# A ten-stage kernel on one core: half splits taken from GpSimd, the convolution's tables in their own tile, the last expert rows in two tiles

## The chip, the cores and the metric

The kernel runs on one core of one Trainium2 chip. Its engines are TensorE (PE in the profile; PEld is its weight load), VectorE (DVE), ScalarE (ACT), GpSimd (POOL) and SyncE (SP), which issues most of the transfers. The metric is the time on the device in microseconds, the median of several runs. Before the change it is 1920.85 us, the median of 1922.42, 1920.85 and 1916.68.

## The reference

One batch of 256 tokens with 1024 features goes through two blocks of two layers each. Everything is float32.

```python
def first_block(x, ...):
    for layer in range(2):
        mix = conv_mixers(x, ...) if layer % 2 == 0 else stick_breaking_attention(x, ...)
        x = layer_norm(DEEPNORM_ALPHA * x + mix, ...)
        ffn = hierarchical_moe(x, ...)   # 32 experts of hidden width 512, 2 of them for each token
        x = layer_norm(DEEPNORM_ALPHA * x + ffn, ...)
    return x

def conv_mixers(x, w_in, conv_a, conv_b_w, conv_b_bias, norm_b_g, norm_b_b, w_out):
    a_b, a_c, a_v, b_val, b_gate = jnp.split(x @ w_in, ...)
    y_a = a_b * causal_depthwise_conv(a_c * a_v, conv_a)              # width 3
    g = b_val * jax.nn.sigmoid(b_gate)
    g = causal_depthwise_conv(g, conv_b_w) + conv_b_bias              # width 31
    y_b = jax.nn.silu(layer_norm(g, norm_b_g, norm_b_b))
    return jnp.concatenate([y_a, y_b], axis=-1) @ w_out
```

The second block does for each of its two layers, with an RMS norm ahead of each part: an attention mixer (layer 0 two kinds of heads, block attention and dilated windows; layer 1 a mixer, NSA, with compressed, selected and windowed keys and values, weighted by gates), a SwiGLU layer of width 2816, and a gated embedding (PLE): `x + sigmoid(norm(x) @ w_gate) * (p @ w_proj)`.

## The kernel before

There are ten stages, one after the other: 0 the convolution mixer, 1 experts, 2 stick-breaking attention, 3 experts, 4 the first attention mixer of the second block, 5 SwiGLU, 6 embedding gate, 7 NSA mixer, 8 SwiGLU, 9 embedding gate and output. By the trace they begin at about 0, 119, 590, 709, 1182, 1297, 1493, 1525, 1697 and 1889 us.

**Weights and halves.** Weights come as items of 1 MB by SyncE's queue (`pump`, L202), each into the next free one of a few rotating buffers. A matmul in float32 is done in three passes (`mm3`, L397 to L399) of operands that were split into a high and a low part, and so each dense item is split before use, half by half. ScalarE copies the high part of a half (`wh`, L237) and `split_to` has the low one (`wl`) subtracted at L248, on GpSimd if the flag `on_pool[0]` is set and else on VectorE:

```python
            eng = G if on_pool[0] else V
            eng.tensor_tensor(out=lv, in0=src, in1=hv.bitcast(F32), op=OP.subtract)
```

**What sets the order.** Each unit of work on one half ends with `tick()`. It first runs whatever was put off to this tick with `later(n, f)`, n ticks after it was put off, and then splits ahead, up to three halves beyond the one in use:

```python
        while due and due[0][0] <= now[0]:
            heapq.heappop(due)[2]()
        split_to(limit(here[0] + 3))
```

Each engine runs its instructions in the order in which this program writes them. Four high and four low tiles rotate.

**Stage 0** (`conv_mix`). One tile `scr` of 128x2048 holds the rows of the convolutions' tables (`fvr`, 37 rows), the rows of all norms' vectors (`vr`, 14 rows) and, later, `yb` and `sq`. SyncE's queue loads them between weight items. TensorE transposes the tables at L601 (`vecs`) and the norms' vectors at L331 (`vectors`); x is transposed at L522.

**Experts** (stages 1 and 3). Each expert's hidden part goes through `ps<-w,xg` (L919) and its output (L941) is written to 32 rows of a tile `y4` that four experts share (`down`, L950 on VectorE and L952 on ScalarE). A last set of matmuls combines the rows of all experts per token (`combine`), and `Rows` normalises: `take` (L495) gathers statistics, `begin` (L499, L458) ends them, `shift` (L504) makes minus mean times rstd, and `end` writes x (L512, L514). At the end of stage 3 `lows` has the first split halves of stage 4 subtracted on GpSimd, and `Norm.put_all` writes `x` in feature order with its high and low parts (L1325, L1246 and L1248, L1251).

**Stage 2** (`stick_mix`) builds a mask from a tile `neg`, which shares its buffer with the tile `kt` of the cumulative masks (L1113).

**Embedding gates** (stages 6 and 9, `ple`). Eight units of one half each: 24 matmuls, then `gate` (L1644 on VectorE, a sigmoid on ScalarE) and, for the unit before, `finish` (L1649, L1650), after every second one the high and low part of x for the next stage (L1251). `on_pool` is set for every second unit.

**NSA mixer** (stage 7). After units for gates, queries and values come two turns of a loop over the head groups g = 2 and 3, with a unit for the group's queries (`q_unit`), steps of the attention of the earlier groups (`step`), and the scale of the queries (`qs`: `hsq`, L1381 to L1385). `on_pool` is set from this loop on until late in the output projection (`feat_out`).

Of the kernel before, what the change touches and what calls it, by code (L numbers as in the profile page):

```python
# [70 lines left out]
def tile_kernel(ctx: ExitStack, tc: tile.TileContext, A, out, first=0, last=9):  # L71
# [197 lines left out]
    due, now = [], [0, 0]  # L269

# [10 lines left out]
    def tick():  # L281
        now[0] += 1
        while due and due[0][0] <= now[0]:
            heapq.heappop(due)[2]()
        split_to(limit(here[0] + 3))
# [193 lines left out]
    class Rows:  # L479
# [17 lines left out]
        def begin(self):  # L497
            self.mv = sm.tile([128, 2], F32, name="lnmv")
            V.bn_aggr(self.mv, self.st)  # L499
            self.r = rstd(self.mv[:, 1:2], LN_EPS, 1.0, "ln")  # L500

        def shift(self):
            self.nb = sm.tile([128, 1], F32, name="lnnb")
            V.scalar_tensor_tensor(self.nb, self.mv[:, 0:1], -1.0, self.r, op0=OP.mult, op1=OP.mult)  # L504
# [50 lines left out]
    def conv_mix():  # L555


        with tc.tile_pool(name="cm", bufs=1, reuse_waits="tile") as cp:
            wd = [c_tile(F32).rearrange("p (n f) -> p n f", f=32) for _ in range(2)]
            xh, xl = take_c(2)  # L560
            scr = cp.tile([128, 2048], F32, name="scr")
            fvr, vr = scr[0:37, 0:512], scr[0:14, 1024:2048]
            yb = scr[:, 1024:2048].rearrange("p (b t) -> p b t", b=4)
            sq = scr[:, 0:1024].rearrange("p (b t) -> p b t", b=4)
            pump(2)
            Q.dma_start(fvr[0:3, :], A["even_conv_a"][0])
            Q.dma_start(fvr[3:34, :], A["even_conv_b_w"][0])
            Q.dma_start(fvr[34:35, :], A["even_conv_b_bias"])
            Q.dma_start(fvr[35:36, :], A["even_norm_b_g"])
            Q.dma_start(fvr[36:37, :], A["even_norm_b_b"])  # L570
            pump(1)
            vectors = vector_loads(vr)
            prep = router_loads(0)
            pump()
            vec = cp.tile([128, 4, 37], F32, name="vec")
# [5 lines left out]
            gs = cp.tile([128, 2, 4, 28 + SEQ], F32, name="gs")  # L581
# [8 lines left out]
            for c in range(2):  # L590
                for kq in range(2):
                    v = turned(c, kq)
                    s = (slice(None), slice(4 * kq, 4 * kq + 4), slice(c * 128, (c + 1) * 128))
                    S.activation(xh[s], v, AF.Copy)
                    V.tensor_tensor(out=xl[s], in0=v, in1=xh[s].bitcast(F32), op=OP.subtract)
                split_to(c + 1)

# [22 lines left out]
            def shifted():  # L620

                for b in range(2):
                    ps = [bank()[:, 0:28 + SEQ] for _ in range(4)]
                    for s in range(4):
                        for c in range(4):
                            f = slice(32 * c, 32 * c + 32)
                            T.matmul(ps[c][32 * s:32 * s + 32], ident[f, f], gp[f, b, s:s + 28 + SEQ], start=True,
                                     stop=True)
                    for c in range(4):
                        if c % 2:  # L630
                            S.activation(gs[:, b, c, :], ps[c], AF.Copy)
                        else:
                            V.tensor_copy(gs[:, b, c, :], ps[c])

            def conv(i):
                ps = bank()
                for b in range(2):
                    for q in range(8):
                        for c in range(4):
                            T.matmul(ps[32 * c:32 * c + 32, b * SEQ:(b + 1) * SEQ], wd[i][:, (b * 4 + c) * 8 + q, :],  # L640
                                     gs[:, b, c, 4 * q:4 * q + SEQ], start=q == 0, stop=q == 7)
                for b in range(2):
                    S.activation(yb[:, 2 * i + b, :], ps[:, b * SEQ:(b + 1) * SEQ], AF.Identity,
                                 bias=vec[:, 2 * i + b, 34:35])
            later(2, vecs)
            later(3, tap_rows)
            later(3, vectors)
# [18 lines left out]
            kept = {}  # L666

            def b_sum():
                m = bank()
                for b in range(4):  # L670
# [5 lines left out]
            def b_stats():  # L676
                p2 = bank()
# [178 lines left out]
    def moe(layer):  # L856
        stage = 2 * layer + 1
        with tc.tile_pool(name="wd", bufs=ND, reuse_waits="tile") as wd, \
# [74 lines left out]
            def down(e):  # L933
# [11 lines left out]
                if ee == 0:  # L945
                    y4s[q] = hl.tile([128, D], F32, name="y4", tag="l")
                for c in range(4):
                    o, v = y4s[q][32 * ee:32 * ee + 32, c * 256:(c + 1) * 256], pd[32 * c:32 * c + 32, 0:256]
                    if e == NE - 1 and c % 2:
# [4 lines left out]
            def combine(q, cs=(0, 1)):  # L954
                for c in cs:
                    for n in range(2):
                        T.matmul(acc[2 * c + n], dwt[:, q % 2, c * 128:(c + 1) * 128],
                                 y4s[q][:, n * 512:(n + 1) * 512], start=q == 0, stop=q == 7)
# [117 lines left out]
            r[0].begin()  # L1076
# [4 lines left out]
            r[1].begin()  # L1081
            r[1].shift()
            r[1].end(dst[1], 1)
            def lows():
                on_pool[0] = True
                split_to(ahead)
# [11 lines left out]
    def stick_mix():  # L1098
        with tc.tile_pool(name="st", bufs=1, reuse_waits="tile") as cp, \
# [4 lines left out]
            neg = cw.tile([128, 128], F32, name="neg", tag="kt", bufs=1)  # L1104
# [128 lines left out]
    class Norm:  # L1233
# [20 lines left out]
        def put_all(self):  # L1254

            for k in (0, 2, 1, 3, 4, 6, 5, 7):
                self.high(k, k % 4 > 1)
            for k in range(8):
# [375 lines left out]
    def ple(cp, cw, pl, cur, nxt):  # L1634
# [18 lines left out]
        for k in range(8):  # L1653
# [7 lines left out]
            on_pool[0] = k % 2 == 1  # L1661
            tick()
        on_pool[0] = False
# [3 lines left out]
    def nsa_mix(bp, sl, cur, nxt):  # L1667
        with tc.tile_pool(name="ns", bufs=1, reuse_waits="tile") as cp, \
# [242 lines left out]
            on_pool[0] = True  # L1911
            for g in (2, 3):
                qs, turn_q = q_unit(g)
# [5 lines left out]
                turn_q()  # L1919
                if g == 2:  # L1920
                    later(1, step)
            step()
            step()
            nx = nxt()
# [134 lines left out]
```

## Time and profile before

| | |
|---|---|
| median of three runs | 1920.85 us |
| the profiled execution's own time | 1922.68 us |
| its span | 1921.0 us |
| mean granted TensorE clock | 0.903 |
| TensorE busy | 1631.7 us, 85% |
| VectorE busy | 740.4 us, 39% |
| ScalarE busy | 677.2 us, 35% |
| GpSimd busy | 122.1 us, 6% |
| moved by DMA | 559 MB, 291 GB/s |

The profile is of one execution. A row of the timeline has its start and its busy time in us, engine, line, operation, output and inputs by name with partitions x elements, and how many like instructions follow each other; the bracket at its end tells how long the engine had stood before it, and for whom. The clock is TensorE's granted clock as a share of its full 2.4 GHz; 0.50 is 1.2 GHz. Shown matmul times overlap, since matmuls are pipelined. The page gives the span in 40 slices of 48 us; here is TensorE's busy share and clock, in tenths, and the DMA engines' share:

```profile
PE   8999667676679998667667679999999998999998
PEclk9999788778879999778778779999999898999999
DMA  9679999999999469999999998535555463145550
```

### The profile page before, as it was taken

What the parts mean: (1) busy time and instruction counts of PE and PEld (TensorE: products, weight loads), DVE (VectorE), ACT (ScalarE), POOL (GpSimd) and SP (SyncE); (2) the same over time, 40 slices, a digit from 0 to 9 for tenths busy, and PEclk for the clock granted to TensorE, in tenths of its full rate; (3) what the DMA queues carried; (4) which work ended last, traced back from release to release, by engine and by line L of the source; (5) the groups of instructions that cost most, each with busy time, mean ns of one, the idle gap of its engine ahead of it and who ended that gap; (6) DMA issues with size and microseconds to landing.
All of it is one profiled execution on the core that took longest, in us unless ns stands there. A gap on an engine that the chain in (4) does not pass through costs nothing. (4 is left out here: it accounts for less than half of the span.)

```text
span 1921.0 us, 35228 instructions
## 1 busy us (share of the span) xinstructions
PE 1631.7 (85%) x15094; PEld 1229.6 (64%) x15094; DVE 740.4 (39%) x1505; ACT 677.2 (35%) x1295; POOL 122.1 (6%) x126
## 2 busy tenths in 40 slices
PE   8999667676679998667667679999999998999998
PEld 7875323233238985324223227989999996799998
DVE  5551000001006661001001006666556757666557
ACT  4422111111116643111111115665444546654445
POOL 0010000000001000000000002100000412210002
PEclk9999788778879999778778779999999898999999
DMA  9679999999999469999999998535555463145550
GB/s 297 234 287 416 419 418 418 420 419 418 418 411 355 172 257 396 418 419 419 419 419 419 417 419 284 161 130 181 198 176 193 128 198 100 56 148 197 189 176 23
DMA packets 236570, 559.06 MB, mean 291 GB/s; under 512 B 15563, under 2 KB 124938, under 8 KB 236408
## 3 DMA queue, kind: packets, MB, share of 16 engines
q1 hardware_dynamic: 226520, 551.59, 75.2%
q10 hardware_dynamic: 9264, 4.97, 0.9%
q8 instruction: 122, 2.00, 0.4%
q14 instruction: 40, 0.33, 0.0%
q0 software_dynamic: 624, 0.18, 0.0%
HBM read 555.55 MB, written 1.15 MB: 290 GB/s over the span
## 5 line engine op out<-in xcount | busy, mean ns | idle before, releaser
L919 PE MATMUL ps<-w,xg 128*32 128x256 f32 x4096 | 366.3, 497 | 233.8 <-DMA w<-in_expert_w_up_dram 232.7
L919 PEld LDWEIGHTS ps<-w,xg 128*32 128x32 f32 x4096 | 135.4, 133 | 447.8 <-DMA w<-in_expert_w_up_dram 266.4
L248 DVE TENSOR_TENSOR wl<-w,wh 128x1024 fp32r<-128x1024 f32 x255 | 310.0, 1228 | 171.8 <-ACT wh L237 168.6
L237 ACT ACTIVATE wh<-w 128x1024 fp32r<-128x1024 f32 x273 | 282.9, 1051 | 91.3 <-PE ps L398 60.3
L923 DVE TENSOR_TENSOR hs<-hs,ps 128x128 f32<-128x128 f32 x64 | 18.4, 288 | 635.5 <-ACT hs L922 635.5
L397 PE MATMUL ps<-xh,wh 128*128 128x256 f32 (+1 forms) x840 | 237.2, 282 | 0.0
L399 PE MATMUL ps<-xh,wl 128*128 128x256 f32 (+1 forms) x840 | 236.3, 281 | 0.8 <-DVE wl L248 0.8
L398 PE MATMUL ps<-xl,wh 128*128 128x256 f32 (+1 forms) x840 | 236.6, 282 | 0.3 <-DVE xl L1251 0.2
L922 ACT ACTIVATE hs<-ps 128x128 f32<-128x128 f32 x64 | 17.8, 278 | 591.6 <-PE ps L919 587.0
L399 PEld LDWEIGHTS ps<-xh,wl 128*128 128x128 f32 (+1 forms) x840 | 159.2, 190 | 1.2 <-DVE wl L248 1.2
L398 PEld LDWEIGHTS ps<-xl,wh 128*128 128x128 f32 (+1 forms) x840 | 159.2, 190 | 1.1 <-DVE xl L1251 1.1
L397 PEld LDWEIGHTS ps<-xh,wh 128*128 128x128 f32 (+1 forms) x840 | 159.3, 190 | 0.0
L941 PE MATMUL ps<-w,ht 128*32 128x256 f32 x2048 | 141.1, 423 | 0.0
L952 ACT ACTIVATE y<-ps 32x256 f32<-32x256 f32 x252 | 94.5, 375 | 119.8 <-PE ps L941 110.1
L941 PEld LDWEIGHTS ps<-w,ht 128*32 128x32 f32 x2048 | 73.1, 126 | 65.4 <-issue 32.1
L399 PE MATMUL ps<-wh,xl 128*128 128x256 f32 x336 | 96.8, 288 | 4.2 <-DVE xl L1251 4.2
L397 PE MATMUL ps<-wh,xh 128*128 128x256 f32 x336 | 99.3, 296 | 0.0
L398 PE MATMUL ps<-al,wh 128*128 128x256 f32 x352 | 99.1, 281 | 0.0
L397 PE MATMUL ps<-ah,wh 128*128 128x256 f32 x352 | 99.1, 281 | 0.0
L399 PE MATMUL ps<-ah,wl 128*128 128x256 f32 x352 | 99.0, 281 | 0.0
L398 PE MATMUL ps<-wl,xh 128*128 128x256 f32 x336 | 96.9, 288 | 0.4 <-DVE wl L248 0.4
L397 PE MATMUL ps<-w,wh 128*128 128x256 f32 x272 | 78.8, 290 | 0.0
(406 smaller groups left out, 2730.4 us busy)
## 6 DMA issues: line engine op xcount, KB each, us to landing
w<-in_expert_w_up_dram SPq DMA_DIRECT2D x256, 1024.0 KB
w<-in_expert_w_down_dram SPq DMA_DIRECT2D x128, 1024.0 KB
w<-in_w_ffn_gate_dram SPq DMA_DIRECT2D x22, 1024.0 KB
w<-in_w_ffn_up_dram SPq DMA_DIRECT2D x22, 1024.0 KB
w<-in_w_ffn_down_dram SPq DMA_DIRECT2D x22, 1024.0 KB
w<-in_odd_w_qkv_dram SPq DMA_DIRECT2D x12, 1024.0 KB
w<-in_w_in_ab_dram SPq DMA_DIRECT2D x12, 1024.0 KB
w<-in_w_in_nsa_dram SPq DMA_DIRECT2D x10, 1024.0 KB
```

The costliest lines, as they stand in the source:

```text
L237: S.activation(hv, src, AF.Copy)
L248: eng.tensor_tensor(out=lv, in0=src, in1=hv.bitcast(F32), op=OP.subtract)
L397: T.matmul(ps, lh, rh, start=start, stop=False, **kw)
L398: T.matmul(ps, lh, rl, start=False, stop=False, **kw)
L399: T.matmul(ps, ll, rh, start=False, stop=stop, **kw)
L919: T.matmul(pu[32 * j:32 * j + 32, 0:256], r, w[:, kk, :, j, :], start=k == 0, stop=k == 7)
L922: S.activation(hs, pu[:, 0:128], AF.Silu)
L923: V.tensor_tensor(out=hs, in0=hs, in1=pu[:, 128:256], op=OP.mult)
L941: T.matmul(pd[32 * c:32 * c + 32, 0:256], hts[e][:, 32 * j:32 * j + 32], w[:, jj, c * 256:(c + 1) * 256], start=j == 0, stop=j == 3)
L952: S.activation(o, v, AF.Copy)
```

## The change

- *Stage 0.* `scr` is gone. `yb`, `fvr`, `vr`, `gs` and `sq` have tiles of their own (`fvr` shares a place with the later `gs`, `vr` with the later `sq`). The five loads of `fvr` move from SyncE's queue to ScalarE's, ScalarE loads its sigmoid table at the start, three weight items go ahead of the norms' rows, `vectors` is put off to the 7th tick instead of the 3rd, and `warm(8)` and `warm(3)` add bfloat16 matmuls of 128x512 whose results aren't used, 8 before x arrives and 3 behind its first half.
- *Experts.* The last four experts' rows go to two tiles, columns 0 to 511 written by ScalarE and 512 to 1023 by VectorE. `begin` makes minus mean on VectorE, and `shift` multiplies it by rstd on ScalarE. At the end of stage 3 one low goes to GpSimd instead of two; `put_all` has the second subtracted on VectorE.
- *Stage 2.* `neg` shares its place with `sh` instead of `kt`.
- *Embedding gates.* All lows are VectorE's.
- *NSA mixer.* Ahead of each of the two turns the lows are made for four halves ahead, on VectorE, and `hold` keeps ticks from splitting during the turn. `on_pool` is set only ahead of the output projection.

```diff
+    hold = [False]
...
-        split_to(limit(here[0] + 3))
+        if not hold[0]:
+            split_to(limit(here[0] + 3))
...
-        def begin(self):
+        def begin(self, shift=False):
             self.mv = sm.tile([128, 2], F32, name="lnmv")
             V.bn_aggr(self.mv, self.st)
+            if shift:
+                self.neg = sm.tile([128, 1], F32, name="lnng")
+                V.tensor_scalar(self.neg, self.mv[:, 0:1], -1.0, None, op0=OP.mult)
             self.r = rstd(self.mv[:, 1:2], LN_EPS, 1.0, "ln")
...
-            V.scalar_tensor_tensor(self.nb, self.mv[:, 0:1], -1.0, self.r, op0=OP.mult, op1=OP.mult)
+            S.activation(self.nb, self.neg, AF.Copy, scale=self.r)
...
-            scr = cp.tile([128, 2048], F32, name="scr")
-            fvr, vr = scr[0:37, 0:512], scr[0:14, 1024:2048]
-            yb = scr[:, 1024:2048].rearrange("p (b t) -> p b t", b=4)
-            sq = scr[:, 0:1024].rearrange("p (b t) -> p b t", b=4)
-            pump(2)
-            Q.dma_start(fvr[0:3, :], A["even_conv_a"][0])
...
-            pump(1)
+            yb = cp.tile([128, 4, SEQ], F32, name="yb")
+            fvr = cp.tile([37, 512], F32, name="fvr", tag="gs")
+            vr = cp.tile([14, D], F32, name="vr", tag="sq")
+            S.dma_start(fvr[0:3, :], A["even_conv_a"][0])
...
+            nc.scalar.preload_act_table_set("sigmoid_and_others")
+            pump(3)
             vectors = vector_loads(vr)
             prep = router_loads(0)
             pump()
+            warm(8)
...
                 split_to(c + 1)
+                if not c:
+                    warm(3)
...
-            later(3, vectors)
+            later(7, vectors)
...
-                    y4s[q] = hl.tile([128, D], F32, name="y4", tag="l")
+
+                    y = [hl.tile([128, D], F32, name="y4", tag="l") for _ in range(1 + (q == 7))]
+                    y4s[q] = [y[0][:, 0:512], y[-1][:, 512:1024]]
...
-                    if e == NE - 1 and c % 2:
+                    if q == 7 and c > 1:
                         V.tensor_copy(o, v)
...
             def lows():
                 on_pool[0] = True
-                split_to(ahead)
+                split_to(stage_half[stage + 1] + 1)
                 on_pool[0] = False
...
-            neg = cw.tile([128, 128], F32, name="neg", tag="kt", bufs=1)
+            neg = cw.tile([128, 128], F32, name="neg", tag="sh")
...
                 self.high(k, k % 4 > 1)
+            split_to(limit(here[0] + 2))
             for k in range(8):
                 self.low(k)
...
-            on_pool[0] = k % 2 == 1
             tick()
-        on_pool[0] = False
...
-            on_pool[0] = True
             for g in (2, 3):
+
+                split_to(limit(here[0] + 4))
+                hold[0] = True
...
                 turn_q()
+                hold[0] = False
...
             step()
             step()
+            on_pool[0] = True
```

In the changed kernel most lines stand some 12 further down. On VectorE at the end of the second expert stage, before (`lnmv`, `lne`, `lnr` and `lnnb` are mean and variance, variance plus epsilon, rstd, and minus mean times rstd):

```order
L499 BN_AGGR lnmv<-lnst 128x2
L458 TENSOR_SCALAR lne<-lnmv 128x1
L504 SCALAR_TENSOR_TENSOR lnnb<-lnmv,lnr 128x1
L512 TENSOR_SCALAR xn<-ps,lnmv,lnr 128x512
L1325 TENSOR_SCALAR x<-ps,fvec 128x128 x8
L1246 TENSOR_SCALAR xh<-x,fvec 128x256 x4
L1251 SCALAR_TENSOR_TENSOR xl<-x,fvec,xh 128x256 x8
```

The same place after (`lnng` is minus mean):

```order
L501 BN_AGGR lnmv<-lnst 128x2
L504 TENSOR_SCALAR lnng<-lnmv 128x1
L460 TENSOR_SCALAR lne<-lnmv 128x1
L517 TENSOR_SCALAR xn<-ps,lnmv,lnr 128x512
L1337 TENSOR_SCALAR x<-ps,fvec 128x128 x8
L1257 TENSOR_SCALAR xh<-x,fvec 128x256 x4
L248 TENSOR_TENSOR wl<-w,wh 128x1024
L1262 SCALAR_TENSOR_TENSOR xl<-x,fvec,xh 128x256 x8
```

`lnnb` has left VectorE, and one low part of a half now stands between the high parts of x and its low parts. On VectorE in the first embedding gate, before (`rb` is the norm's factor, `pp` the projected embedding):

```order
L1644 TENSOR_TENSOR act<-rb,ps 128x256
L1649 TENSOR_TENSOR act<-act,pp 128x256
L1650 TENSOR_TENSOR x<-x,act 128x256
L1644 TENSOR_TENSOR act<-rb,ps 128x256
L1649 TENSOR_TENSOR act<-act,pp 128x256
L1650 TENSOR_TENSOR x<-x,act 128x256
L248 TENSOR_TENSOR wl<-w,wh 128x1024
```

The same place after:

```order
L1656 TENSOR_TENSOR act<-rb,ps 128x256
L1661 TENSOR_TENSOR act<-act,pp 128x256
L1662 TENSOR_TENSOR x<-x,act 128x256
L248 TENSOR_TENSOR wl<-w,wh 128x1024
L1656 TENSOR_TENSOR act<-rb,ps 128x256
```

A low stands behind each unit instead of each second one. On GpSimd in the NSA mixer from the loop over the groups to its output projection, before (`hrs` is the rstd of the heads):

```order
L1385 TENSOR_TENSOR hrs<-hss,expo 128x8 x3
L248 TENSOR_TENSOR wl<-w,wh 128x1024 x2
L1385 TENSOR_TENSOR hrs<-hss,expo 128x8
L248 TENSOR_TENSOR wl<-w,wh 128x1024 x2
L1385 TENSOR_TENSOR hrs<-hss,expo 128x8
L248 TENSOR_TENSOR wl<-w,wh 128x1024 x5
```

The same place after (`ssum` sums the squares of the next norm):

```order
L1397 TENSOR_TENSOR hrs<-hss,expo 128x8 x5
L248 TENSOR_TENSOR wl<-w,wh 128x1024 x6
L1291 TENSOR_TENSOR ssum<-sq 128x256
L1296 TENSOR_TENSOR ssum<-ssum,sq 128x256 x4
```

No low stands between the steps of `hrs` any more, and six instead of five follow them.

## Rows read from the trace of the kernel before

**Rows 1.** Waits: engine, output, line, for whom; us in total, times, longest.

```profile
PE ps L919 <- DMA w<-in_expert_w_up_dram: 232.7, 193, 4.7
```

**Rows 2.** Windows: length, PE, PEld, DVE, ACT, POOL busy, clock, DMA share, GB/s.

```profile
60.00:90.00 30.00, 29.32 (x312) 25.79 (x311) 13.84 (x25) 12.42 (x22) 1.63 (x1) 1.00 0.40 145
136.00:577.00 441.00, 316.49 (x3438) 149.84 (x3438) 42.50 (x131) 72.30 (x196) 3.44 (x6) 0.81 1.02 415
```

**Rows 3.** One line's instructions: ns min/median/max, first and last start.

```profile
L1383 DVE TENSOR_SCALAR hss<-hss x14: 171/171/2279, 1185.6 to 1625.5; 128x8 f32<-128x8 f32 x14
...
L1649 DVE TENSOR_TENSOR act<-act,pp x16: 417/420/2562, 1501.3 to 1915.7; 128x256 f32<-128x256 f32 x16
...
L1650 DVE TENSOR_TENSOR x<-x,act x16: 424/426/2515, 1503.6 to 1916.1; 128x256 f32<-128x256 f32 x16
```

**Rows 4.** Timeline of POOL, stages 6 and 7.

```profile
1512.21 1.38 POOL L1279 TENSOR_TENSOR ssum<-sq 128x256 f32<-128x256 f32 x1 [2.75 <-ACT sq L1277]
...
1600.11 4.66 POOL L248 TENSOR_TENSOR wl<-w,wh 128x1024 fp32r<-128x1024 f32 x2 [13.99 <-ACT wh L237]
```

**Rows 5.** Timeline of DVE, stage 6.

```profile
1517.66 0.87 DVE L1251 SCALAR_TENSOR_TENSOR xl<-x,fvec,xh 128x256 fp32r<-128x256 f32 x2
1518.45 1.22 DVE L248 TENSOR_TENSOR wl<-w,wh 128x1024 fp32r<-128x1024 f32 x1
```

**Rows 6.** Windows of stages 0, 6 and 7 (columns as in Rows 2).

```profile
19.00:25.70 6.70, 6.62 (x35) 6.36 (x35) 2.77 (x10) 3.83 (x10) 0.00 (x0) 0.50 0.40 81
1509.00:1520.60 11.60, 11.58 (x97) 11.36 (x95) 11.26 (x19) 7.34 (x13) 5.96 (x5) 1.00 0.33 103
1525.20:1537.70 12.50, 12.50 (x60) 12.50 (x60) 4.94 (x7) 4.42 (x7) 3.41 (x9) 0.50 0.37 108
1607.40:1612.60 5.20, 5.20 (x25) 3.64 (x26) 4.99 (x29) 3.58 (x14) 0.00 (x0) 0.50 0.15 38
```

**Rows 7.** Timeline of PE, stage 0.

```profile
8.09 1.97 PE L522 MATMUL ps<-ident,x 128*128 128x128 f32 x8 [1.59 <-DMA x<-in_x_dram]
9.90 2.08 PE L409 MATMUL ps<-w,wh 128*128 128x256 f32 x8
...
19.08 0.61 PE L601 MATMUL ps<-ident,scr 37*128 37x37 f32 x4 [2.30 <-DMA scr<-in_norm_mix_dram]
```

**Rows 8.** Timeline of PE, end of the second experts.

```profile
1170.34 1.06 PE L522 MATMUL ps<-ident,xn 128*128 128x128 f32 x8 [2.23 <-DVE xn L512]
```

**Rows 9.** Timeline of SP, stage 0.

```profile
23.31 9.59 SPq L202 DMA_DIRECT2D w<-in_even_w_in_dram  x5
```

**Rows 10.** Timeline of DVE, start of stage 2 and end of the second experts.

```profile
585.18 2.64 DVE L1125 TENSOR_SCALAR xf<-ps,fvec 128x128 f32<-128x128 f32 x8 [0.57 <-POOL ntri L1113]
...
1161.77 0.43 DVE L950 COPY y<-ps 32x256 f32<-32x256 f32 x1 [0.44 <-ACT y L952]
...
1167.19 2.29 DVE L504 SCALAR_TENSOR_TENSOR lnnb<-lnmv,lnr 128x1 f32<-128x1 f32 x1 [0.72 <-POOL lnr L460]
...
1173.91 5.19 DVE L1251 SCALAR_TENSOR_TENSOR xl<-x,fvec,xh 128x256 fp32r<-128x256 f32 x8
```

**Rows 11.** Timeline of ACT, start of stage 2.

```profile
588.72 1.15 ACT L1128 ACTIVATE w<-xf 128x512 fp32r<-128x512 f32 x2
```

**Rows 12.** Timeline of PE, starts behind stands in stages 6 and 7.

```profile
1524.81 0.58 PE L399 MATMUL ps<-wh,xl 128*128 128x256 f32 x1 [4.23 <-DVE xl L1251]
...
1607.38 1.51 PE L1472 MATMUL ps<-jdent,sS 128*128 128x128 f32 x6 [5.31 <-DVE sS L1465]
```

**Rows 13.** Timeline of DVE, the two turns of stage 7.

```profile
1602.53 2.27 DVE L1383 TENSOR_SCALAR hss<-hss 128x8 f32<-128x8 f32 x1
...
1625.46 2.28 DVE L1383 TENSOR_SCALAR hss<-hss 128x8 f32<-128x8 f32 x1
```

**Rows 14.** Windows of stages 7 and 9 (columns as in Rows 2).

```profile
1645.00:1690.00 45.00, 42.25 (x335) 33.38 (x332) 25.70 (x120) 26.12 (x80) 11.87 (x5) 1.00 0.22 71
1893.00:1914.00 21.00, 21.00 (x182) 21.00 (x181) 16.44 (x25) 9.44 (x16) 5.13 (x2) 1.00 0.07 22
```

## What the change was predicted to do

> **What bounds the kernel now.** I read the busy slices of the page first: TensorE is busy in nine tenths of most slices, least where the experts run. The waits come next: TensorE's largest by far is for expert weights, 232.7 us in 193 waits [rows 1]. Then windows, one for each regime: in the first expert stage the DMA engines are full (share 1.02, 415 GB/s) and TensorE is busy 316 of 441 us, while just before it the same queues stand at 0.40 with a busy TensorE [rows 2]. So outside the two expert stages time is gained or lost where TensorE stands still, or runs at half clock. Last, timelines of one engine at each place of the diff; the reader is to look for the bracket behind a TensorE row (how long it stood, for whom) and for an instruction that takes far longer than its like.
>
> Two things recur. A VectorE instruction beside a GpSimd half split takes the split's time: L1383 has a median of 0.171 us and a longest of 2.279, L1649 0.420 and 2.562, L1650 0.426 and 2.515 [rows 3]; two splits on GpSimd take 4.66 us [rows 4] and one on VectorE 1.22 [rows 5]. And after each stand of TensorE follows a stretch at 0.50 of the clock (1.2 GHz of 2.4), 5 to 13 us long [rows 6].
>
> **The change part by part.** All is summed against the profiled execution's own 1922.7 us, 0.1% above the median of 1920.85.
>
> *Stage 0: -6.6.* TensorE stands 2.30 us at L601 for the rows that share one tile with the norm's rows [rows 7]; with a tile of their own, loaded from ScalarE's queue ahead of the weights, they are there. That is -2.3. The 6.7 us behind that stand run at 0.50 [rows 6]; at full clock they take half, -3.35. Third, TensorE starts cold: the first eight L522 take 1.97 us [rows 7], against 1.06 for eight of the same form later [rows 8], and the eight L409 behind them 2.08. The eight added 512-column warm matmuls fill the wait for x; ScalarE's copies of the transposed halves limit what comes of it, so I take 1.0, between 0 and 1.9. L331 is only moved. ScalarE issues five DMAs and a table load first; they are over before x's second half comes at 8.09, and the table load in mid-stage goes. The third weight item goes out ahead of the norm's rows; the later items are issued at 23.31 as before [rows 9], well ahead. Bounds: 2.3 (the clock stays low, nothing from the warm start) and 7.6. It passes through the expert stage if the first expert weights go out as much earlier: at share 0.40 the queue waits for free buffers, not for the DMA engines [rows 2], and these come free by TensorE's work.
>
> The Trainium skill (DMA: Bandwidth & Descriptors, Rules for kernel authors) says that another issuing engine doesn't add bandwidth, since all use the same 16 DMA engines. By it the `fvr` rows, 75 KB, would delay x by an estimated 0.2 us at the 415 GB/s of [rows 2], and this term would be 6.4; no run here shows it alone.
>
> *End of the first experts: -0.4.* ScalarE and VectorE write the last rows of y in turns, because they share a tile: VectorE's 0.43 copy stands 0.44 for ScalarE's [rows 10]. Four such in a row are 1.7 us; two tiles make it two beside two, -0.85. The longer VectorE turn delays the gather of `ht` by about half a copy, 0.25, and the new negation (about 0.17, as L1383 alone [rows 3]) lies on the chain: -0.4 net, between -0.9 and +0.3.
>
> *Stage 2, `neg`: 0.* VectorE's 0.57 wait goes [rows 10], but TensorE starts when ScalarE's second split copy (588.72) is through its first half [rows 11], and VectorE's eight moves end before that. Between 0 and -0.57.
>
> *End of the second experts: -2.0.* As above -0.4. L504 takes 2.29 us here, beside GpSimd's split [rows 10]. On ScalarE no row shows a 128x1; the nearest are 0.17 for a small VectorE instruction [rows 3] and 0.58 for ScalarE's 128x512 [rows 11], and I take 0.2: -2.1 of TensorE's 2.23 wait for xn [rows 8]. What is late next: the second low, now 1.22 on VectorE ahead of the eight xl (5.19 us [rows 10]), of which TensorE has the wl passes to hide half: +0.6; -0.1 for a shorter xl beside one split fewer. Between -0.5 and -2.9.
>
> *Stage 6 into 7: -9.7.* TensorE stands 4.23 us for the last xl [rows 12], as VectorE's L1649 and L1650 take 2.5 us four times. Without splits on GpSimd that goes, 4 x 2.1 = 8.4, and four lows come, 4 x 1.22 = 4.9 [rows 5]. VectorE's work in two gate units is then 2 x (3 x 0.42 + 1.22) + 0.87 = 5.8 us, the last being two xl [rows 3, 5]; TensorE's for the same is 97 matmuls in 11.6 us [rows 6], 48 of them 5.7. So VectorE just keeps up and the stand shrinks to about 1: with the 0.2 before the row -3.5. The 12.5 us behind it run at 0.50; without the stand I take them at full clock, -6.2. Bounds: -2.5 (VectorE a unit late, the clock falls) and -10.4.
>
> *Stage 7: -4.2.* Both `hss` chains meet a split on GpSimd: L1383 takes 2.27 and 2.28 instead of 0.17 [rows 13], and TensorE stands 5.31 for the softmax behind the first [rows 12]. With `hold` no split runs there: 2 x 2.1 = -4.2. The lows now made beforehand (one more on VectorE ahead of g=2, two ahead of g=3) lie beside TensorE's q unit. Were they in the chain they would give back 3 x 1.22 = 3.7. If in turn the clock stays up over the 5.2 us at 0.50 [rows 6], 2.6 more. From -0.5 to -6.8.
>
> *Stage 9: 0.* TensorE is busy 21.00 of 21.00 us [rows 14]: VectorE's turns don't show. Between -0.5 and +1.
>
> Sum: 6.6 + 0.4 + 0 + 2.0 + 9.7 + 4.2 + 0 = 22.9, so 1922.7 - 22.9 = 1899.8. All upper ends: 7.6 + 0.9 + 0.6 + 2.9 + 10.4 + 6.8 + 0.5 = 29.7, 1893; all lower ends: 2.3 - 0.3 + 0 + 0.5 + 2.5 + 0.5 - 1 = 4.5, 1918.
>
> **The rivals.** *The clock falls anyway at stage 6.* VectorE's 5.8 against 5.7 us a pair leaves no slack, and GpSimd's adds of the squares remain beside it: the one shown takes 1.38 us [rows 4], and what stretches it can hold VectorE as well. A stand of 2 us is then enough: the three shown, of 2.30 us and more [rows 7, 12], each had its stretch at 0.50 [rows 6]. So 6.2 of the clock and 1 of the stand do not come: 1907.0. Against it: four stretched instructions go, worth more than the four lows.
>
> The Trainium skill (SBUF — State Buffer, Who interferes with whom) bears on this rival: a VectorE instruction with two inputs in SBUF and a GpSimd one that reads SBUF shut each other out for a whole instruction. It speaks against this change, for a moved low has two such inputs and GpSimd's five adds are such readers; the trace agrees so far that it is whole instructions that are shut out.
>
> *Stage 0's gain is lost in the experts,* if the DMA stream, full for 441 us, doesn't start earlier [rows 2]: 1899.8 + 6.6 = 1906.4. For it, the share of 1.02; against it, the 0.40 before.
>
> *VectorE swallows it.* Ten lows of 1.22, 12.2 us, come to the engine on which TensorE's stands end. If both late stages remain VectorE's, only 2.3 of stage 0, 2.4 at the experts and 1 at the entry are left, 5.7: 1917.0.
>
> *Slower: stage 7's out-projection starts with too little in store.* During `hold` TensorE uses up what was split, and two halves stand ready where there were three; `on_pool` starts just then, so two lows follow each other on GpSimd, 4.66 us [rows 4], beside the softmax of the last groups on VectorE. If the second comes later than TensorE needs it, each of six halves comes late by some 1.5 us, two thirds of a low there, 9 us, and TensorE, busy 42.25 of 45.00 at full clock there [rows 14], runs about half of it at 0.50, +20: 1899.8 + 29 = 1929. Decisive is whether TensorE reaches the second half within some 5 us of the first tick. Against it: between these halves lie the attention's matmuls and their stands, so it should take longer.
>
> **How the numbers follow.** The forecast as summed 0.52 (its own range 1893 to 1903); the clock 0.20; the experts 0.12; VectorE 0.10; slower 0.06. The range goes from the upper ends less 2 for the spread of the runs, 1891, past the first two rivals together, 1899.8 + 7.2 + 6.6 = 1913.6, to 1914; outside are the last two rivals. A measurement of this kernel tells 0.3%, 5.8 us, from no change: faster is below 1915.1, slower above 1926.6. Faster hold the forecast and the first two rivals, 0.84, and a little of the third, 0.86; same the rest of it and of mishaps, 0.08; slower 0.06.
>
> **What would show it right or wrong.** Right: no stand of 2 us at L601 and the granted clock at 1.00 between 19 and 26; the first expert wait some 6 us earlier; L504's successor on ScalarE below 0.3; no L1649 or L1650 above 1 us and a stand below 1.5 at stage 7's entry with 1.00 behind it; L1383 at 0.17 in all 14. Wrong: a low clock after the entry (first rival); DMA share no longer 0.40 before the experts yet the same end (second); stands for wl or x where VectorE is busy throughout (third); TensorE waiting for wl of L248 on GpSimd in the out-projection (slower).

## The result and the profile after

The changed kernel takes 1929.03 us (median of six, 1927.84 to 1932.83), the kernel before 1919.24 (six runs): a ratio of 1.0056, with a 95% interval from 1.0040 to 1.0071. It is slower by 10 us where 21 us less were forecast, and it lies outside the forecast range of 1891 to 1914 us. The profiled execution took 1932.58 us, with a span of 1930.5.

Most of the stands that the prediction spoke of went as it said. TensorE after, in stage 0 (beside [rows 7]), at the end of the second experts ([rows 8]) and at the entry and in the first turn of stage 7 ([rows 12]):

```profile
4.73 1.06 PE L527 MATMUL ps<-ident,x 128*128 128x128 f32 x8
10.88 1.77 PE L527 MATMUL ps<-ident,x 128*128 128x128 f32 x8 [4.43 <-DMA x<-in_x_dram]
19.21 0.44 PE L608 MATMUL ps<-ident,fvr 37*128 37x37 f32 x4
1190.87 1.04 PE L527 MATMUL ps<-ident,xn 128*128 128x128 f32 x8
1199.76 0.50 PE L437 MATMUL ps<-wh,xl 128*128 128x256 f32 x2 [0.37 <-DVE xl L1262]
1200.63 1.29 PE L437 MATMUL ps<-wh,xl 128*128 128x256 f32 x6 [0.37 <-DVE xl L1262]
1546.52 0.38 PE L401 MATMUL ps<-wh,xl 128*128 128x256 f32 x1 [1.39 <-DVE xl L1262]
1619.98 1.07 PE L1484 MATMUL ps<-jdent,sS 128*128 128x128 f32 x6 [1.94 <-DVE sS L1477]
```

The stand at L608 is gone, that of 2.23 for xn is gone, 4.23 became 1.39 and 5.31 became 1.94. New are 4.43 us for x at 10.88, where it came at 8.09 before, and two stands for xl of 0.37. The lines that GpSimd's splits had stretched (ns min/median/max, beside [rows 3]):

```profile
L1395 DVE TENSOR_SCALAR hss<-hss x14: 171/172/173, 1206.7 to 1637.0; 128x8 f32<-128x8 f32 x14
...
L1661 DVE TENSOR_TENSOR act<-act,pp x16: 409/419/634, 1525.9 to 1925.3; 128x256 f32<-128x256 f32 x16
```

L1395 is never stretched any more, and of the two lines that took 2.5 us none reaches 1 us (L1661 at most 0.63, L1662, the old L1650, 0.84).

One stand is new at the end of both expert stages. The condition for VectorE's copies, `q == 7`, holds for the last four experts and no longer for the last one alone, so two copies of the last expert but one stand ahead of the gather of `ht` (L937), for which the last expert's matmuls wait: the bracket names nobody, but they start 0.1 us after `ht` is there. TensorE before, TensorE after and VectorE after, at the end of the first expert stage:

```profile
573.83 0.33 PE L928 MATMUL ps<-ident,hs 128*128 128x128 f32 x1
...
589.40 1.26 PE L409 MATMUL ps<-w,wh 128*128 128x256 f32 x8 [1.84 <-ACT w L1128]
```

```profile
581.52 0.33 PE L935 MATMUL ps<-ident,hs 128*128 128x128 f32 x1
...
583.73 1.93 PE L948 MATMUL ps<-w,ht 128*32 128x256 f32 x32 [1.02 <-issue]
...
598.02 1.93 PE L411 MATMUL ps<-w,wh 128*128 128x256 f32 x8 [1.97 <-ACT w L1139]
```

```profile
582.44 0.86 DVE L960 COPY y<-ps 32x256 f32<-32x256 f32 x2 [1.92 <-ACT y L962]
583.34 0.29 DVE L937 COPY ht<-ps 128x128 f32<-128x128 f32 x1
```

From the last expert's transpose to the first matmul of stage 2 it is 15.57 us before and 16.50 after. The rest of the time is lost in the stream of weights. Windows of the kernel after (columns as in [rows 2]):

```profile
60.00:90.00 30.00, 29.32 (x311) 25.79 (x310) 14.79 (x26) 13.08 (x22) 1.63 (x1) 1.00 0.49 186
200.00:500.00 300.00, 205.89 (x2059) 92.31 (x2059) 23.85 (x66) 41.01 (x113) 0.00 (x0) 0.77 1.02 409
800.00:1100.00 300.00, 204.53 (x2066) 92.32 (x2070) 24.12 (x67) 41.28 (x114) 0.00 (x0) 0.77 1.02 409
1201.50:1203.50 2.00, 2.00 (x15) 2.00 (x14) 2.00 (x2) 2.00 (x4) 0.00 (x0) 0.72 0.70 200
1203.50:1212.00 8.50, 8.50 (x51) 8.50 (x51) 5.64 (x12) 1.68 (x2) 2.37 (x2) 0.66 0.44 138
1547.00:1559.50 12.50, 12.50 (x107) 12.30 (x106) 6.22 (x11) 6.39 (x11) 3.43 (x9) 1.00 0.59 188
```

and of the kernel before, in the middle of its expert stages:

```profile
200.00:500.00 300.00, 204.69 (x2116) 92.32 (x2112) 25.01 (x69) 42.78 (x118) 0.00 (x0) 0.79 1.02 419
800.00:1100.00 300.00, 208.13 (x2112) 92.61 (x2112) 25.01 (x69) 43.38 (x119) 0.00 (x0) 0.77 1.03 419
```

The DMA engines are as busy as before (1.02 to 1.03) and move 409 GB/s instead of 419, in both expert stages. Each stage of some 440 us bound by the stream is longer by 440 x (419/409 - 1) = 10.8 us, the two by 21.5. In the trace's records of single packets the 4 KB packets of expert weights between 200 and 500 us take 159 ns in 92 of 100 cases before, and in 15 of 100 after, with a mean of 163.5. The waits say the same: 245.5 us of TensorE for expert weights, against 232.7 [rows 1], and 285.8 against 266.4 of its weight load:

```profile
PE ps L926 <- DMA w<-in_expert_w_up_dram: 245.5, 185, 5.1
```

### The profile page after: what moved, and what is told of

Its sections match the earlier page's. It is cut to its first block, busy times and chain, and to the rows that moved or that the text cites. A ratio compares the mean times of both kernels' runs of the same rounds, so it can differ in the third digit from the quotient of the medians.

```text
span 1930.5 us, 35245 instructions
## 1 busy us (share of the span) xinstructions
PE 1638.0 (85%) x15105; PEld 1230.7 (64%) x15105; DVE 741.2 (38%) x1527; ACT 672.4 (35%) x1286; POOL 97.2 (5%) x116
## 5 line engine op out<-in xcount | busy, mean ns | idle before, releaser
L926 PE MATMUL ps<-w,xg 128*32 128x256 f32 x4096 | 364.7, 494 | 246.5 <-DMA w<-in_expert_w_up_dram 245.5
L926 PEld LDWEIGHTS ps<-w,xg 128*32 128x32 f32 x4096 | 135.1, 131 | 456.8 <-DMA w<-in_expert_w_up_dram 285.8
L248 DVE TENSOR_TENSOR wl<-w,wh 128x1024 fp32r<-128x1024 f32 x265 | 321.9, 1226 | 177.5 <-ACT wh L237 173.1
L948 PE MATMUL ps<-w,ht 128*32 128x256 f32 x2048 | 152.4, 449 | 2.1 <-issue 2.1
L962 ACT ACTIVATE y<-ps 32x256 f32<-32x256 f32 x240 | 90.0, 375 | 131.6 <-PE ps L948 124.7
L948 PEld LDWEIGHTS ps<-w,ht 128*32 128x32 f32 x2048 | 78.5, 133 | 73.7 <-issue 45.8
```

Source lines behind the costliest of these rows:

```text
L926: T.matmul(pu[32 * j:32 * j + 32, 0:256], r, w[:, kk, :, j, :], start=k == 0, stop=k == 7)
L948: T.matmul(pd[32 * c:32 * c + 32, 0:256], hts[e][:, 32 * j:32 * j + 32], w[:, jj, c * 256:(c + 1) * 256], start=j == 0, stop=j == 3)
L962: S.activation(o, v, AF.Copy)
```

## The experiments

**Why is the stream slower?** Nothing in the change touches the expert weights. But `lnng` is a new small tile, of 32 bytes in each of two buffers, in the pool `sm`, and that pool lies ahead of all weight buffers: each starts 64 bytes further on. By the placing of the tiles, before, the 7 buffers of the first pool start 224 bytes beyond a multiple of 256 and the 13 others on one; after, 32 and 64 beyond. Two runs take the shift apart from the rest.

The kernel before with the shift alone:

```diff
+    gap = ctx.enter_context(tc.tile_pool(name="gap", bufs=1))
+    gap.tile([128, 16], F32, name="gap")
     sm = ctx.enter_context(tc.tile_pool(name="sm", bufs=2))
```

> The kernel before with an unused gap of 64 bytes per partition ahead of the small tiles, so that every weight buffer starts 64 bytes further on, as in the changed kernel; nothing else differs. Address theory (the DMA stream of the expert stages is slower, 409 instead of 419 GB/s, because of where the buffers start): about 1941 us, 1920 and some 21 us for two expert stages, 408 to 410 GB/s between 200 and 500 us. Rival (the slower stream comes from what the changed kernel does, its loads on ScalarE's queue or its order of items, or from the chip and not from the addresses): 1917 to 1923 us and 418 to 420 GB/s.

Measured: 1942.8 us, 1.0117 of before (1.0100 to 1.0134). An unused gap of 64 bytes costs 22 us.

The changed kernel without the shift:

```diff
-                self.neg = sm.tile([128, 1], F32, name="lnng")
-                V.tensor_scalar(self.neg, self.mv[:, 0:1], -1.0, None, op0=OP.mult)
+                self.nb = sm.tile([128, 1], F32, name="lnnb")
+                V.tensor_scalar(self.nb, self.mv[:, 0:1], -1.0, None, op0=OP.mult)
...
-            self.nb = sm.tile([128, 1], F32, name="lnnb")
-            S.activation(self.nb, self.neg, AF.Copy, scale=self.r)
+            S.activation(self.nb, self.nb, AF.Copy, scale=self.r)
```

> The changed kernel, but minus mean and minus mean times rstd share one tile (the activation works in place), so that the added pair of small tiles of 64 bytes is gone and every weight buffer starts where it did before. Address theory: 419 GB/s, and 1929 - 21 = 1908 us (1904 to 1912). Rival (orders, queues): 409 GB/s and 1929 us (1927 to 1933).

Measured: 1908.42 us, 0.9941 of before (0.9925 to 0.9958). So the shift costs 1929.0 - 1908.4 = 20.6 us, and the rest of the change gains 12.1 (before 1920.48 in these runs). The two runs of the 20.6 were not made side by side; pad128_after below, which was run beside after_in_place, lies 20.2 above it. The windows 200 to 500 us, first of pad64_before, then of after_in_place:

```profile
200.00:500.00 300.00, 203.41 (x2071) 90.78 (x2066) 23.83 (x66) 41.01 (x113) 0.00 (x0) 0.78 1.02 409
```

```profile
200.00:500.00 300.00, 207.60 (x2116) 93.66 (x2112) 25.02 (x69) 43.28 (x119) 0.00 (x0) 0.78 1.03 419
```

**Which starts are fast?** The same gap with 32 bytes in the kernel before, 128 bytes in the changed one, and 224 bytes in the kernel before:

```diff
+    gap.tile([128, 8], F32, name="gap")      # pad32_before
+    gap.tile([128, 32], F32, name="gap")     # pad128_after
+    gap.tile([128, 56], F32, name="gap")     # pad224_before
```

> The kernel before with a gap of 32 bytes: the 7 buffers of the first pool now start on a multiple of 512 bytes (before 480 beyond one), the 13 others 32 beyond a multiple of 256 (before on one). Address theory in its plainest form (what starts on a multiple of 256 is fast): mixed, 7 of 20 buffers fast, 411 to 414 GB/s and 1930 to 1938 us. If any shift off the old addresses is slow: 409 and 1941. Rival (not the addresses): 1917 to 1923.

> The changed kernel with a gap of 128 bytes, 192 beyond the addresses of before. Address theory: slow as the changed kernel, 409 GB/s and 1929 us (1925 to 1933), unless only some residues are slow, then 419 and 1908. Rival (not the addresses): 1929.

> The kernel before with a gap of 224 bytes: the 7 buffers of the first pool start 192 bytes beyond a multiple of 256, the 13 others 224 beyond one (before 224 and 0). If 0 and 224 are fast and 32, 64, 160 and 192 slow, as the runs so far have it: 7 of 20 items slow, 415 to 416 GB/s, 1927 us (1924 to 1931). If every address but the old ones is slow: 409 GB/s, 1942 us.

Measured: 1925.73 us (1.0027, 1.0015 to 1.0038) at 415 GB/s; 1928.59 (1.0047) at 409; 1940.76 (1.0102, 1.0086 to 1.0117) at 409. With 32 bytes the 7 first buffers start on a multiple of 256 and 13 don't: less was lost than I expected. With 224 bytes I expected 415 to 416 and was wrong: 224 beyond a multiple is slow as 32, 64, 160 and 192 are. The same windows of the three, in the same order:

```profile
200.00:500.00 300.00, 205.64 (x2096) 92.77 (x2096) 25.00 (x69) 43.30 (x119) 0.00 (x0) 0.78 1.02 415
```

```profile
200.00:500.00 300.00, 207.01 (x2071) 92.47 (x2063) 23.84 (x66) 41.02 (x113) 0.00 (x0) 0.76 1.03 409
```

```profile
200.00:500.00 300.00, 204.67 (x2071) 91.00 (x2063) 23.78 (x66) 40.99 (x113) 0.00 (x0) 0.77 1.03 409
```

That the 7 first buffers of the kernel before start 224 beyond a multiple hardly shows: its slow packets, 8 of 100, come where several items in a row go to these seven, as the order of the items has it. With the packets of the first expert stage counted off in that order, 256 for an item, an item that stands alone or in a pair among the seven has 1 to 3 of 100 packets over 160 ns; the third and the fourth in a row of four have 20 and 62. Starts 96 and 128 bytes beyond a multiple were not tried, so these runs don't tell whether a multiple of 128 would be enough.

That made a rule with one free test: put all 20 buffers on a multiple of 256. The pool of the router's tables has 1312 bytes, 32 more than five times 256; ahead of the first weight pool instead of behind it, it makes up the missing 32 there and leaves the 13 other weight buffers where they were.

```diff
+    first_mp = ctx.enter_context(tc.tile_pool(name="mp", bufs=1, reuse_waits="tile"))
     wa = ctx.enter_context(tc.tile_pool(name="wa", bufs=NA))
...
-            rt["pool"] = es.enter_context(tc.tile_pool(name="mp", bufs=1, reuse_waits="tile"))
+            rt["pool"] = first_mp
```

> The kernel before with that pool moved alone. Theory: 420 to 421 GB/s, 1917 us (1915 to 1919). Rival: 409 GB/s, 1941 us; or no difference, 1920.

Measured: 1916.92 us, 0.9983 of before (0.9973 to 0.9993), at 420 GB/s; 99.8 of 100 packets take 159 ns.

```profile
200.00:500.00 300.00, 210.71 (x2116) 94.66 (x2120) 24.98 (x69) 43.38 (x119) 0.00 (x0) 0.77 1.03 420
```

**Why does stage 0 gain 2 us instead of 6.6?** x's second half comes 2.8 us late. In the packets, the 31 rows of the wide convolution on ScalarE's queue are 31 packets of 2 KB, one after another, most of 84 to 115 ns, over some 3.5 us, together at the rate of one engine. That x's rows on that engine share it with them is inferred: the trace doesn't say on which engine a packet ran. Two ways out, in the changed kernel without its shift: the tables back on SyncE's queue behind two items, or the 31 rows in two transfers.

```diff
-            S.dma_start(fvr[3:34, :], A["even_conv_b_w"][0])
...
-            pump(3)
+            pump(2)
+            Q.dma_start(fvr[3:34, :], A["even_conv_b_w"][0])     # and the four others likewise
+            pump(1)
```

> The changed kernel without its 64-byte shift (as after_in_place), and the five loads of the convolutions' tables issued by SyncE behind two weight items, as before, instead of by ScalarE at the start. Theory (these small rows, issued first, hold up the second half of x): TensorE's second x transposes start near 8.1 us instead of 11.1, stage 0 ends 2 to 4 us earlier than in after_in_place, 1905 us (1903 to 1907). Rival (x is late because of the third weight item or the issue order on SyncE, or the stage absorbs it): start near 11, 1908 (1907 to 1911).

Measured: 1909.92 us, 0.9951 (0.9937 to 0.9966): no gain. The first half of the theory holds, the second doesn't: x comes 2.4 us earlier (8.71 instead of 11.11), but now the tables come late, and the old stand is back. It also shows what that stand was for. The tables have a tile of their own here, and their packets run from 14.8 to 17.9 us; in the kernel before, where they share one with the norm's rows, they run from 14.7 to 17.9. So it is their place in SyncE's queue that makes TensorE stand, and not the shared tile, though the bracket names the norm's rows in both.

```profile
8.71 1.09 PE L526 MATMUL ps<-ident,x 128*128 128x128 f32 x8 [2.08 <-DMA x<-in_x_dram]
...
19.07 0.61 PE L608 MATMUL ps<-ident,fvr 37*128 37x37 f32 x4 [3.12 <-DMA vr<-in_norm_mix_dram]
```

```diff
-            S.dma_start(fvr[3:34, :], A["even_conv_b_w"][0])
+            S.dma_start(fvr[3:19, :], A["even_conv_b_w"][0, 0:16])
+            S.dma_start(fvr[19:34, :], A["even_conv_b_w"][0, 16:31])
```

> The changed kernel without its 64-byte shift (as after_in_place), and the 31 rows of the wide convolution loaded on ScalarE's queue as two transfers of 16 and 15 rows instead of one of 31. Theory (31 rows go one after another through one DMA engine, and x's rows on that engine wait behind them): TensorE's second x transposes start near 8.1 us instead of 11.1, no wait at L608, stage 0 ends 3 to 5 us earlier, 1904 us (1902 to 1907). Rival (stage 0 is then bound by the arrival of the weight items): a later wait for w, 1907 to 1910.

Measured: 1906.76 us, 0.9920 (0.9906 to 0.9933).

```profile
8.27 1.09 PE L526 MATMUL ps<-ident,x 128*128 128x128 f32 x8 [1.23 <-DMA x<-in_x_dram]
...
26.21 2.17 PE L635 MATMUL ps<-gp,ident 32*32 32x284 f32 x64 [1.74 <-DVE gp L665]
```

Both early arrivals at once, and no stand at L608; one of 1.74 us for `gp` is new behind them. The first matmul of the router (L852 in the kernel before) starts at 126.2 us instead of 129.3 in after_in_place and 131.0 before; of the 4.8 us against before, 3.8 are left at the last expert's transpose (570.01 instead of 573.83) and 2.8 when the first expert stage ends (last write of x by L514 at 581.1 instead of 583.9), the last 1.0 being lost around the stand of 1.02 above. Another execution of the same stage 0, that of best below, starts the router at 128.0 and ends the stage at 582.8. By the medians it is 1.7 us, at the edge of what these runs can tell.

**What does the low on VectorE cost at the entry of stage 4?** The two stands of 0.37 us, and behind them a clock of 0.72 and 0.66 in the windows above: 0.74 + 0.28 x 2.0 + 0.34 x 8.5 = 4.2 us in that execution. Both lows back on GpSimd, again without the shift:

```diff
-                split_to(stage_half[stage + 1] + 1)
+                split_to(ahead)
...
-            split_to(limit(here[0] + 2))
             for k in range(8):
                 self.low(k)
```

> The changed kernel without its 64-byte shift, and at the end of the second expert stage both first lows on GpSimd again, as before, and none on VectorE between the high and low parts of x. Theory (the low on VectorE makes TensorE stand twice 0.4 us for xl, and the clock falls to 0.50 behind that): no stand for xl, granted clock 1.00 from 1174 to 1190, and stage 4 starts 3 to 4 us earlier: 1904.5 us (1903 to 1907). Rival (GpSimd's second low stretches VectorE's high parts of x by up to 1 us, the stands come back, the clock falls just so): 1908 (1907 to 1911).

Measured: 1907.3 us, 0.9941 (0.9925 to 0.9956), not told apart from after_in_place's 1908.4 by the times, and so a miss: 3 to 4 us were forecast. In the profile one stand of 0.37 is left and the clock stays up, where in after_in_place (second fence) it falls.

```profile
1174.00:1182.00 8.00, 7.55 (x60) 7.04 (x60) 7.88 (x10) 5.65 (x7) 3.45 (x6) 1.00 1.01 315
1182.00:1190.00 8.00, 8.00 (x69) 8.00 (x69) 5.22 (x12) 2.60 (x3) 2.38 (x3) 1.00 0.61 188
```

```profile
1174.00:1182.00 8.00, 7.25 (x41) 6.56 (x40) 7.17 (x11) 5.01 (x6) 2.75 (x4) 0.76 0.97 299
1182.00:1190.00 8.00, 8.00 (x58) 8.00 (x57) 4.88 (x11) 2.60 (x3) 1.84 (x2) 0.81 0.61 195
```

The other profiles show that this isn't fixed. Behind the two stands the clock has a mean of 0.67 over 10.5 us in four of them (after, after_in_place, tables_on_sync, tables_spread) and 1.00 in the fifth, pad128_after; behind the one stand it is 1.00 in three (entry_lows_pool and, below, both_undone and best) and 0.84 in the fourth, aligned_best. The windows of pad128_after and aligned_best:

```profile
1201.00:1211.50 10.50, 10.50 (x90) 10.50 (x90) 7.80 (x14) 5.24 (x7) 2.38 (x2) 1.00 0.60 179
```

```profile
1176.40:1186.90 10.50, 10.50 (x77) 10.50 (x77) 7.80 (x14) 5.43 (x7) 2.37 (x2) 0.84 0.54 167
```

The kernel with both the tables on SyncE's queue and the lows on GpSimd:

> The changed kernel without its 64-byte shift, with both of the above: tables by SyncE, both lows on GpSimd. Theory: the gains add, 1908.4 - 3 - 3.5 = 1902 us (1899 to 1904). Rival (one of them is hidden by the expert stage's stream or the other): 1905 to 1908.

Measured: 1908.34 us, 0.9945 (0.9931 to 0.9959): a miss, as tables_on_sync was, beside which it lies 1.6 us lower.

**The two parts for the late stages, each alone in the kernel before.** First the embedding gates:

```diff
-            on_pool[0] = k % 2 == 1
             tick()
-        on_pool[0] = False
```

> The kernel before with one part of the change alone: all lows of the embedding gates on VectorE. Forecast of the prediction: the stand of 4.23 us for xl at the entry of stage 7 shrinks to about 1 us and the 12.5 us behind it run at full clock, -9.7: 1920.5 - 9.7 = 1911 us (1909 to 1913). Rival (VectorE too full, the clock falls again): 1917 us (1916 to 1919).

Measured: 1916.4 us, 0.9982 (0.9972 to 0.9993), -3.6 where -9.7 were forecast. Then the NSA part of the change as it stands:

```diff
-            on_pool[0] = True
             for g in (2, 3):
+                split_to(limit(here[0] + 4))
+                hold[0] = True
...
                 turn_q()
+                hold[0] = False
...
+            on_pool[0] = True
             nx = nxt()
```

> The kernel before with one part of the change alone: in stage 7 the lows made ahead of each of the two turns, none in them, and GpSimd's from the output projection on. Forecast of the prediction: -4.2, 1915.8 us (1914 to 1918). Rival of the prediction (too little split ahead of the output projection): 1929 us or, in part, 1921 and more.

Measured: 1914.56 us, 0.9963 (0.9950 to 0.9977), -6.0 where -4.2 were forecast. The entry of stage 7 with the stand as before (hold_alone, timeline and window), and without it (gate_lows_alone):

```profile
1524.74 0.58 PE L401 MATMUL ps<-wh,xl 128*128 128x256 f32 x1 [4.19 <-DVE xl L1253]
...
1525.20:1537.70 12.50, 12.50 (x98) 12.30 (x98) 5.41 (x9) 5.27 (x10) 3.41 (x9) 0.91 0.53 159
```

```profile
1525.43 0.39 PE L399 MATMUL ps<-wh,xl 128*128 128x256 f32 x1 [1.39 <-DVE xl L1251]
...
1525.80:1538.30 12.50, 12.50 (x107) 12.30 (x106) 6.21 (x11) 6.39 (x11) 3.43 (x9) 1.00 0.62 192
```

**A version that beats both.** The changed kernel in place, with the tables in two transfers and both lows on GpSimd, and then the same with every weight buffer on a multiple of 256:

> As tables_spread, and both first lows of stage 4 on GpSimd as in entry_lows_pool. Theory: both gains, no stand behind x's arrival and the clock at 1.00 behind the second expert stage, 1902 us (1900 to 1905), clear of both kernels. Rival (what stage 0 gains is lost behind the expert weights): 1907.

> The kernel of best, with the pool of the router's tables (1312 bytes) placed ahead of the first pool of weight buffers instead of behind it: all 20 weight buffers then start on a multiple of 256 bytes, no byte more is used. Theory (what doesn't start on a multiple of 256 is slower; in the kernel before and in best 7 of 20 buffers don't): the last slow items go, 420 to 421 GB/s, and 2 to 4 us less than best, 1902 us (1900 to 1904). Rival (any address but those of before is slow): 409 GB/s, 1925 us.

Measured: 1905.1 us, 0.9917 (0.9903 to 0.9930), and 1903.39, 0.9912 (0.9894 to 0.9931); these runs don't tell the two apart. best lies 1.7 us below tables_spread, which was run beside it. The second is 17.5 us faster than the kernel before (1920.92 beside it) and some 25 faster than the changed one.

## Why the prediction was wrong

*The step that failed* is one that the prediction did not take: its sum holds the expert stages at their old length and only asks whether stage 0's gain gets through them, so that what the change itself does to the stream stands at nothing, without a reason. The added pair of `lnng` was priced as an instruction (0.17 us) and not as a place in memory. Its 64 bytes cost 20.6 us (pad64_before: 22.3), about as much as the whole forecast gain. None of the four rivals was this one. The rival of a slower kernel has 1929 us, which is what was measured, but only the number agrees: its out-projection has no stand for a low on GpSimd. The step could have been weighed: the Trainium skill (DMA: Bandwidth & Descriptors, How a descriptor splits into AXI transactions) says that a transaction must begin at an address that is a multiple of 256 bytes, and that a transfer from elsewhere fetches unused bytes ahead of its start. By that page 4 KB would take 17 of them instead of 16, and an estimated 6% would be lost. The measurement decides: the packets lose 2.8% (163.5 against 159 ns), and the stream 2.4%.

*Stage 0, -6.6.* The stand is gone, and the clock is 1.00 at 19 to 25.7 us, as forecast ([rows 6, 7]). But the stand was put down to the tile that the tables share with the norm's rows, and tables_on_sync shows that the own tile alone doesn't take it away. The 3.35 us of clock behind it came from one execution: seven profiles have this stage as before, with a stand of 1.4 to 2.6 us, and the 6.7 us behind it run at 0.50 in two, 0.75 in three and 1.00 in two. Here gate_lows_alone and pad32_before:

```profile
18.92:25.62 6.70, 6.62 (x45) 6.45 (x46) 3.78 (x12) 4.16 (x10) 0.00 (x0) 0.75 0.41 74
```

```profile
18.33:25.03 6.70, 6.58 (x58) 6.37 (x59) 5.24 (x13) 4.06 (x10) 0.00 (x0) 1.00 0.47 97
```

And the loads from ScalarE's queue were costed by their bytes, 0.2 us, and hold up x by 2.8, since the largest goes at the rate of one DMA engine. With them goes most of the warm start: behind its wait of 4.43 us x's second half takes 1.77 us, and 1.09 in tables_spread, where it comes early. Measured 1.7 in after_in_place at the router's start, 4.8 with the rows spread (3.0 in best). The Trainium skill (DMA: Bandwidth & Descriptors, Rules for kernel authors), whose line on queues I had weighed, says in another line of the same table that the outermost dimension sets how many engines a transfer uses; the trace agrees for 31 rows. The rival by which the gain is lost in the experts was right in small part: 1 of the 4.8 us stays in the stream.

*End of the first experts, -0.4.* It became +0.9 (16.50 against 15.57 us). The delay of `ht` was seen and put at half a copy, 0.25; it is two copies, and TensorE stands 1.02 us, in every profile with the two tiles and in none without. The same stand is at the end of the second experts.

*End of the second experts, -2.0.* -2.1 for L504 came as said (its successor on ScalarE takes 0.29). Against it stand the 1.02 us for `ht` and the low ahead of xl: put at +0.6, it costs 0.74 of stands and, where the clock falls behind them, some 3.5 more. By the times its removal gave 1.1 to 1.7 us, at the edge of what they tell. I had held this mechanism for possible at the wrong place, stage 7.

*Stage 6 into 7, -9.7.* This is the largest term of the sum. The stand was forecast at about 1 us and is 1.39, and the clock stays at 1.00 behind it. The term was too large all the same, 3.6 measured alone: its 6.2 us of clock came from one execution. With the same stand of 4.19 us, hold_alone shows 0.91 in the window in which the profile of before has 0.50 [rows 6], which is worth 1.1 us instead of 6.2; and behind stands of 4.18 to 4.23 us the same 12.5 us have 0.86, 0.86, 0.88 and 0.89 in pad32_before, pad224_before, pad64_before and aligned_before (shown). The 2.8 by which the stand shrank and this 1.1 make 3.9, about what was measured.

```profile
1524.00:1536.50 12.50, 12.50 (x96) 12.30 (x96) 5.31 (x8) 5.03 (x9) 3.42 (x9) 0.89 0.51 154
```

The prediction's "after each stand" doesn't hold in its own trace either: behind the 2.23 us for xn [rows 8] the clock of before is 1.00 from 1170.3 to 1180.3 us.

*Stage 7, -4.2.* 6.0 measured alone, within the bounds given; L1395 takes 0.17 in all 14. The rival of too little in store did not happen: TensorE's longest stand in the out-projection is 1.04 us for the softmax at 1672.62, as it was before.

*Stage 9 and `neg`*: nothing to be seen. In all, gates 3.6 and hold 6.0 make 9.6 of the 12.1 us, if the parts add; the other 2.5, for stage 0 and the two ends of the experts together, were not measured alone.

## What to carry to other kernels

A tile that is added costs its place too: look at where it moves the buffers that a bandwidth-bound stage fills, and keep those on a multiple of 256 bytes, which was fast in every run here, for instance with the small pools' sizes or order. Count the rows of a small load, not its bytes: 31 rows held up x by 2.8 us in one piece, and in two of 16 and 15 they cost nothing to be seen. Of a stand for a DMA, look when the bytes arrive and not only at the name in the bracket. A stretch of low clock behind a stand is one execution's; take its size from several profiles before it becomes the largest term of a sum.

## What was not expected of the hardware

- Where buffers start decides 2.4% of a full DMA stream: 409 GB/s with every start off a multiple of 256 bytes, 415 with 13 of 20 off, 419 with 7 of 20 off, 420 with none. 7 of 20 cost so little because one or two such items in a row stay fast there; the slow packets come from the third in a row on. Why that is so is open.
- What the clock does behind a stand differs from one execution to the next. A stand of 4.2 us was followed by 12.5 us at 0.50 in one profile and at 0.86 to 0.91 in five; one of 1.4 to 2.6 us by 6.7 us at 0.50, 0.75 or 1.00; two stands of 0.37 us within 1 us of each other by 10.5 us at a mean of 0.67 in four profiles and at 1.00 in one; one of 0.37 alone by 1.00 in three and 0.84 in one.
